# Hymba-style layer: sample rows and the first sparse keys emitted among the last forgetting-attention blocks, two small copies issued by GpSimd

## The chip, the cores and the metric

The kernel runs on one core of a Trainium2 chip. The metric is device time in microseconds of one execution; the times shown are three executions, and the profile is one further execution of the same program. Engines are named as in the profile: PE (TensorE), PEld (its weight loads), DVE (VectorE), ACT (ScalarE), POOL (GpSimd), SP (SyncE, which here only issues DMAs).

## The reference, cut to what matters

One inference step of one layer. A prompt of 1,024 tokens and 64 sample tokens (8 rows of a batch, 8 tokens each, with 512 cached tokens a row in pages) go through one input projection, whose columns feed two groups of 8 heads. Then:

```python
# group A, sparse attention: compressed, selected and window branches, gated
oa = gates[..., 0:1] * o_c + gates[..., 1:2] * o_s + gates[..., 2:3] * o_w
# group B, forgetting attention: softmax with a per-head decay bias
s = einsum('bqhd,bkhd->bhqk', q, k) * HEAD_DIM ** -0.5 + (cq - ck)
ob = einsum('bhqk,bkhd->bqhd', masked_softmax(s, k_pos <= q_pos), v)
y = x + concat(oa * silu(za), ob * silu(zb)) @ w_out
```

The sample rows do the same with their cached pages (selected-block, window and forgetting pages) in front of the new tokens. With 1,024 tokens and 16 blocks the selected branch covers all causal blocks, so both prompt attentions are dense causal ones; the window branch sees 512 tokens back.

## The kernel before, in words

Values are split in a high and a low 16-bit part, so a product takes two or three matmuls. The work runs in this order, with overlaps: the input projection in 15 chunks of columns; forgetting attention ("fox") over 8 heads, each in two halves of 512 queries; sparse attention ("nsa") over 8 tiles of 128 queries; the 8 sample rows; the output projection.

A fox half is `fox_attend` (lines 762 to 789): for each key block, two matmuls to a score bank (L774, L775), a mask (L777), the exponent on ACT (L711), its high part on ACT (L714), its low part on DVE or, every fifth time, POOL (L716), and the product with the values on PE (L724 to L726). `fox_max` (L757) finds the row maxima ahead of each half; it reads `km` and `qm`, which SP's queue copies from `k1` and `q1` (L703, L704). The first six heads have the last chunks of the input projection as filler between blocks; the last three halves ((6,1), (7,0), (7,1)) come after it and are emitted without filler.

A sparse tile is `nsa_tile`: `nsa_keys` and `nsa_queries` of the next tile (load `kn` or `nq` by SP, scale and split on ACT and POOL, transpose on PE, copy out of PSUM on ACT to `k1a` or `nq1`, then a DMA from there to `kma` (L1035) or `nqm` (L1051)), `nsa_max` (L1073 to L1088), `nsa_attend` (L1117 to L1125) and `nsa_compressed`. A sample row b is `sample_nsa`, `sample_nsa_out`, `sample_fox` and `sample_fox_out` (L1264 to L1371): page loads by SP (0.5 + 0.5 MB for nsa, 2 MB for fox), transposes (L1276, L1334), scores (L1284, L1344), softmax, product (L1304, L1360). It is cut into steps; `fill(rate)` pulls `rate` steps on average after each key block.

Each engine runs its instructions in the order in which they stand in its queue and waits on semaphores. That order is not the order of the text: a scheduler inside the tile framework places instructions by its own estimate of time, with program order and `high_priority` as the preference. A tile's memory comes from pools; a pool that takes over the memory of another (`SC.close()`) makes its first writers wait until the last readers of the old tiles are done. Before, `kma` and `k1a` lie in memory that the fox tiles hold to the end.

Of the kernel before, what the change touches and what calls it, by code (L numbers as in the profile page):

```python
# [22 lines left out]
NT = 8  # L23
T = 1024
# [69 lines left out]
def layer_kernel(ctx, tc, a, o):  # L94
# [633 lines left out]
    def put_max(m, rows, q, cols):  # L728

        n = m.shape[1]  # L730
        mh = B2.tile([128, 2, n], F16, name="mh")
# [15 lines left out]
    def fox_max(h, c):  # L747
        i = h % 2
        mst = B2.tile([128, 2, 4], F32, name="mst")
        m = mst[:, c]  # L750
        for x in range(4):
            t = 4 * c + x
            for s in range(c + 1):
                k0, k1_ = 4 * s, min(4 * s + 4, t + 1)
                n = (k1_ - k0) * 128
                p = PM.tile([128, 512], F32, name=bank["smax"][0], bufs=bank["smax"][1])
                nc.tensor.matmul(p[:, :n], qm[i][0:67, t * 128:(t + 1) * 128], km[i][0:67, k0 * 128:k0 * 128 + n],  # L757
                                 start=True, stop=True)
# [235 lines left out]
    C6 = S3.enter_context(tc.tile_pool(name="nsc", bufs=1, reuse_waits="tile"))  # L994
    BE = B3 = S3.enter_context(tc.tile_pool(name="nsl", bufs=1, reuse_waits="tile"))
    B2 = BN
    cvb = B3.tile([128, 130], F32, name="cvb")
    nc.gpsimd.memset(cvb, 0.0)
    for g in range(2):
        nc.scalar.activation(cvb[64 * g:64 * g + 63, 65 * g:65 * g + 65], cv_p[:, g], AF.Copy)  # L1000
# [4 lines left out]
    nc.gpsimd.memset(kmc, 0.0)  # L1005
    nc.gpsimd.memset(k1c, 0.0)
    stair = BN.tile([128, NT, 64], BF16, name="stair", bufs=1)
    nc.gpsimd.dma_start(stair, a["c_stair"])
    nc.sync.dma_start(kma[64:88].rearrange("p k n -> p (k n)"), a["c_kind"][:, 0:4 * T])
    for g in range(2):  # L1010
        nc.sync.dma_start(kmc[64:88, g, 64 * g:64 * g + 64], a["c_kind"][:, 4 * T:4 * T + 64])
    stairt = B3.tile([128, T], BF16, name="stairt")
    nc.gpsimd.dma_start(stairt, a["c_stairt"])

    def turned(t):
        return PM.tile([128, 512], F16, name="smax", bufs=SMAX)
# [4 lines left out]
        nc.gpsimd.tensor_sub(lo, src, hi)  # L1021

    def nsa_keys(t):
        ks = B2.tile([128, 4, 128], F16, name="nks", bufs=1)
        kn = B2.tile([128, 4, 64], F32, name="kn")
        nc.sync.dma_start(flat(kn[:, 0:2]), outs["slc"][0][t * 128:(t + 1) * 128, 0:128])
        nc.sync.dma_start(flat(kn[:, 2:4]), p_win[(t - 4) * 128:(t - 3) * 128, 0:128] if t >= 4 else kpark[t])
        split16(kn, nsc[:, 0:1], ks[:, :, 0:64], ks[:, :, 64:128])
        p = turned(t)
        for i in range(4):  # L1030
            nc.tensor.transpose(p[:, i * 128:(i + 1) * 128], ks[:, i], ident16)
        pk = p.rearrange("p (i n) -> p i n", i=4)
        c = slice(t * 128, (t + 1) * 128)
        nc.scalar.activation(k1a[:, :, c], pk, AF.Copy)
        nc.sync.dma_start(kma[0:64, :, c], k1a[0:64, :, c])  # L1035

    def nsa_queries(t):
        q = B2.tile([128, 8, 64], F32, name="nq", bufs=1)
        nc.sync.dma_start(q.rearrange("p h d -> p (h d)"), qpark[t])
        qsp = B2.tile([128, 8, 128], F16, name="nqs", bufs=1)  # L1040
        split16(q, nsc[:, 1:2], qsp[:, :, 64:128], qsp[:, :, 0:64])
        r = []
        for g in range(2):
            p = turned(t)
            for i in range(4):
                nc.tensor.transpose(p[:, i * 128:(i + 1) * 128], qsp[:, 4 * g + i], ident16)
            q1 = B2.tile([128, 512], F16, name="nq1", bufs=4)
            qm = B2.tile([128, 512], F16, name="nqm", bufs=4)
            nc.gpsimd.memset(qm[64:88], 0.0)
            nc.scalar.activation(q1, p, AF.Copy)  # L1050
            nc.sync.dma_start(qm[0:64], q1[64:128])  # L1051
            r.append((q1, qm))
        return r

    def nsa_max(g, t, qm):
        m = B2.tile([128, 3, 4], F32, name="nm")
        m2 = B2.tile([128, 2, 4], F32, name="nm2")
        for k in range(2):
            lo = 0 if k == 0 else max(0, t - 4)
            rem = (t + 1 - lo) % 4  # L1060
# [29 lines left out]
        put_max(m.rearrange("p k r -> p (k r)"), 64, qm, slice(0, 512))  # L1090

    def nsa_branch(po, k, g, t, oa):
        l = B2.tile([128, 2, 4], F32, name="nl")
# [38 lines left out]
    def nsa_compressed(t, qq, oa):  # L1132
# [26 lines left out]
    qq = nsa_queries(0)  # L1159
    csp = BN.tile([64, 2, 128], F16, name="csp", bufs=1)  # L1160
    nc.vector.memset(csp, 0.0)
    split16(ck_p, nsc[0:63, 0:1], csp[0:63, :, 0:64], csp[0:63, :, 64:128])
    p = turned(0)
    for g in range(2):
        nc.tensor.transpose(p[:, g * 64:(g + 1) * 64], csp[:, g], ident16[0:64, 0:64])
    for g in range(2):
        z = slice(64 * g, 64 * g + 64)
        nc.scalar.activation(k1c[:, g, z], p[:, z], AF.Copy)
        nc.scalar.activation(kmc[0:64, g, z], p[0:64, z], AF.Copy)
    nsa_keys(0)  # L1170
    nsa_max(0, 0, qq[0][1])
    nsa_max(1, 0, qq[1][1])


    S5 = ctx.enter_context(ExitStack())
# [245 lines left out]
    early[0] = False  # L1421
    rate = 1.5
    mixed[0] = 1
    for t in range(5):
        qq = nsa_tile(t, qq)
    for _ in filler:
        pass
# [188 lines left out]
```

## Time and profile before

| | |
|---|---|
| median of 3 executions | 989.49 us (984.81 to 993.89) |
| the profiled execution, its own time | 983.02 us |
| its span, first to last instruction | 981.2 us |
| mean granted PE clock | 0.984 |
| busy in the span | PE 907.3 us (92%), DVE 636.7 (65%), ACT 611.9 (62%), POOL 383.7 (39%) |
| chain that ended last | PE 68%, DVE 8%, DMA 7%, ACT 5%, issue 3%, POOL 3% |

Busy time is a sum over the whole span. The table of stretches among the rows further down gives it for a part of the span: the length of a stretch less PE's busy time is what PE stood idle there. The profile's PEclk is the granted clock as a share of full speed (1.00 is the level of 2.4 GHz, 0.5 that of 1.2 GHz; a value between is a mix over the stretch).

### The profile page before, as it was taken

To read this page: it belongs to the slowest core of one execution; us is meant where nothing else is said; L and a number is where in the kernel's file an instruction comes from. 1 tells how busy PE (TensorE), PEld (TensorE's weight loads), DVE (VectorE), ACT (ScalarE), POOL (GpSimd) and SP (SyncE) were. 2 spreads that over 40 slices of the span, in tenths; PEclk is the share of its full clock that TensorE was granted. 3 is DMA by queue.
4 is the path that set the end of the run, shared out by engine and by line. 5 is a ranking of instruction groups with operands and counts; after the bars stand their busy time and mean duration, and the time that the engine had idled before them with its cause. 6 is when DMAs were issued, how large, how long until landed. Compare 5 with 4: busy or idle time off the path is not lost.

```text
span 981.2 us, 24638 instructions
## 1 busy us (share of the span) xinstructions
PE 907.3 (92%) x9097; PEld 709.6 (72%) x9097; DVE 636.7 (65%) x1843; ACT 611.9 (62%) x1328; POOL 383.7 (39%) x546
## 2 busy tenths in 40 slices
PE   4898999999999999999997879889999988999997
PEld 3687889878888988877885546556666655677775
DVE  5764666664555426778777736878777888777461
ACT  6854643433454655797876677778898967455430
POOL 4544657754676333343414112334232246311000
PEclk9999999999999999999999999999999999999999
DMA  7563323332333432242215636455345333332241
GB/s 264 141 152 103 94 72 99 108 64 62 98 116 100 127 96 80 88 130 58 76 43 138 194 81 192 155 163 176 120 132 170 97 104 101 97 102 84 85 130 65
DMA packets 122425, 111.74 MB, mean 114 GB/s; under 512 B 39144, under 2 KB 103312, under 8 KB 122280
## 3 DMA queue, kind: packets, MB, share of 16 engines
q1 hardware_dynamic: 121296, 108.52, 37.1%
q0 software_dynamic: 576, 1.05, 0.6%
q8 instruction: 71, 1.16, 0.5%
q10 hardware_dynamic: 432, 0.59, 0.2%
q14 instruction: 50, 0.41, 0.1%
HBM read 79.57 MB, written 27.41 MB: 109 GB/s over the span
## 4 chain that ended last, share of the span: by engine, by line
PE 68%; DVE 8%; DMA 7%; ACT 5%; issue 3%; POOL 3%; SPq 1%; ACTq 0%; DVEq 0%; POOLq 0%
PE acc L245 25%; PE ctr L1502 7%; PE sa L474 3%; PE acc L238 3%; PE pv L724 2%; PE pv L726 2%; PE pv L725 2%; PE st L1117 2%; PE smax L1073 2%; PE st L1118 2%; DMA wst<-in_w_in_dram 2%; PE smax L757 1%; PE st L774 1%; PE ctr L1550 1%; PE st L775 1%
## 5 line engine op out<-in xcount | busy, mean ns | idle before, releaser
L245 PE MATMUL acc<-wsp,xth 128*128 128x256 f16 (+1 forms) x1920 | 335.0, 275 | 5.9 <-ACT xth L175 3.2
L245 PE MATMUL acc<-wsp,xtl 128*128 128x256 f16 (+1 forms) x960 | 264.2, 275 | 0.0
L245 PEld LDWEIGHTS <-xth 128*128 128x128 f16 x1920 | 187.0, 99 | 34.8 <-ACT xth L175 3.8
L1122 ACT ACTIVATE pf<-st,nsc 128x512 f32<-128x512 f32 x132 | 98.8, 781 | 35.2 <-PE st L1118 16.8
L245 PEld LDWEIGHTS <-xtl 128*128 128x128 f16 x960 | 94.5, 98 | 14.8 <-issue 1.4
L724 PEld LDWEIGHTS <-phi 128*128 128x128 f16 x816 | 77.3, 97 | 17.7 <-issue 5.5
L726 PEld LDWEIGHTS <-plo 128*128 128x128 f16 x816 | 77.2, 100 | 11.5 <-DVE plo L716 2.9
L725 PEld LDWEIGHTS <-phi 128*128 128x128 f16 x816 | 77.3, 98 | 3.2 <-issue 0.5
L1123 ACT ACTIVATE phi<-pf 128x1024 f16<-128x1024 f32 (+1 forms) x76 | 71.5, 951 | 12.9 <-PE pv L725 8.0
L711 ACT ACTIVATE pf<-st,nsc 128x512 f32<-128x512 f32 (+1 forms) x96 | 62.9, 669 | 16.0 <-PE st L777 5.8
L1125 DVE TENSOR_TENSOR plo<-pf,phi 128x1024 f16<-128x1024 f32 (+1 forms) x56 | 64.8, 1159 | 8.9 <-ACT phi L1123 8.7
L264 POOL TENSOR_TENSOR nss<-nss,nhalf 128x4 f32<-128x4 f32 (+3 forms) x72 | 68.4, 950 | 4.4
L1125 POOL TENSOR_TENSOR plo<-pf,phi 128x1024 f16<-128x1024 f32 (+1 forms) x20 | 37.2, 1859 | 77.4 <-ACT phi L1123 71.6
L716 DVE TENSOR_TENSOR plo<-pf,phi 128x512 f16<-128x512 f32 (+3 forms) x77 | 51.9, 680 | 22.2 <-ACT phi L714 20.3
L724 PE MATMUL pv<-va,phi 128*128 128x65 f16 x528 | 60.0, 194 | 3.7 <-DVE nt L1102 1.8
L201 ACT ACTIVATE vsq<-wst 128x512 f16<-128x512 f32 (+2 forms) x72 | 40.2, 560 | 33.6 <-DMA wst<-in_w_in_dram 32.9
L725 PE MATMUL pv<-va,phi 128*128 128x64 f16 x528 | 59.9, 196 | 0.0
L726 PE MATMUL pv<-va,plo 128*128 128x65 f16 x528 | 57.5, 193 | 0.2 <-POOL plo L1125 0.2
L714 ACT ACTIVATE phi<-pf 128x512 f16<-128x512 f32 (+1 forms) x96 | 48.7, 523 | 7.8 <-PE pv L726 6.5
L1073 PE MATMUL smax<-kma,nqm 88*128 88x512 f16 (+3 forms) x192 | 48.9, 314 | 4.8 <-DVE nm L1082 2.0
L744 DVE CUSTOM_DVE_ANT_0 junk<-smax,maskw,nm 128x512 bf16<-128x512 f32 x64 | 47.7, 746 | 6.3 <-PE smax L1073 4.1
L1117 PE MATMUL st<-nqm,kma 88*128 88x512 f16 x132 | 50.2, 380 | 0.5 <-ACT pf L1122 0.4
(454 smaller groups left out, 2352.4 us busy)
## 6 DMA issues: line engine op xcount, KB each, us to landing
wst<-in_w_in_dram SPq DMA_DIRECT2D x56, 256.0 KB
sfk<-in_cache_fox_kv_dram SPq DMA_DIRECT2D x32, 256.0 KB
sfv<-in_cache_fox_kv_dram SPq DMA_DIRECT2D x32, 256.0 KB
out_dram<-kv SPq DMA_DIRECT2D x52, 128.0 KB
xin<-in_x_prompt_dram SPq DMA_DIRECT2D x8, 512.0 KB
cpair<-in_cache_nsa_cmp_kv_dram SPq DMA_DIRECT2D x64, 64.0 KB
zpark<-z SPq DMA_DIRECT2D x32, 128.0 KB
spg<-in_cache_nsa_slc_kv_dram SPq DMA_DIRECT2D x32, 128.0 KB
```

The source lines that it names most:

```text
L245: nc.tensor.matmul(ps[:, :n], x[:, k, t * 128:(t + 1) * 128], w[k // 2][:, i, k % 2, :n], start=(k == 0 and j == 0), stop=(k == KT - 1 and ...
L264: nc.gpsimd.tensor_tensor(ss[:n, 0, :h], ss[:n, 1, :h], nhalf[:n, :h], op=ALU.pow)
L711: nc.scalar.activation(p[:n, :cols], ps[:n, :cols], AF.Exp, bias=nsc[:n, 3:4], scale=nsc[:n, 6:7])
L724: nc.tensor.matmul(po[:, s, 0:65], hi[:, c], v[:, 0:65], start=f, stop=False, skip_group_check=True)
L725: nc.tensor.matmul(po[:, s, 0:64], hi[:, c], v[:, 65:129], start=False, stop=False, skip_group_check=True)
L726: nc.tensor.matmul(po[:, s, 0:65], lo[:, c], v[:, 0:65], start=False, stop=l, skip_group_check=True)
L1073: nc.tensor.matmul(pr[:, r], qm[0:88, (r0 + r) * 128:(r0 + r + 1) * 128], kma[0:88, 2 * k + g, j0 * 128:j1 * 128], start=r == 0, stop=not ...
L1117: nc.tensor.matmul(ps, kma[0:88, 2 * k + g, c], qm[0:88], start=True, stop=False)
L1122: nc.scalar.activation(pf[:, 512 * x:512 * x + 512], ps, AF.Exp, bias=nsc[:, 3:4], scale=nsc[:, 2:3])
L1123: nc.scalar.activation(hi[:, 0:n], pf[:, 0:n], AF.Copy)
L1125: (nc.gpsimd if turn[0] % share[mixed[0]] == 0 else nc.vector).tensor_sub(lo_[:, 0:n], pf[:, 0:n], hi[:, 0:n])
L1502: nc.tensor.matmul(ps, l[:, k], w[:, k, c], start=(k == 0 and j == 0), stop=(k == KT - 1 and j == 2))
```

## The change

Four things. (1) The last three fox halves are no longer emitted first at high priority: the sample constants and the first two sample steps come ahead of them, then 0.9 sample steps are pulled after each of their 20 key blocks, and also after each block of the sparse tiles (1.5 before). (2) The keys and queries of sparse tile 0 (`nsa_first`) are emitted behind half (6,1), their maxima behind `fox_early(7)`, ahead of half (7,1). For that `kma`, `k1a` and the small tiles move to pools on the side of memory that is free when the input projection ends. (3) The copies to `kma` and `nqm`, and three loads of constants, are issued by POOL instead of SP. (4) Four sparse tiles, not five, are emitted ahead of the output weights. Two score banks that sample steps borrowed at first are no longer borrowed.

```diff
-        put_max(m, 96, qm[i], slice(512 * c, 512 * c + 512))
+        put_max(m, 96, qm[i], slice(512 * c, 512 * c + 512), B2)
...
+    C6 = ctx.enter_context(tc.tile_pool(name="nsc", bufs=1, side="right", reuse_waits="tile"))
...
-    with tc.high_priority(offset=250):
-        fox_attend(6, 1)
-        fox_early(7)
-        fox_attend(7, 1)
-    SC.close()
...
-    nc.sync.dma_start(kma[64:88].rearrange("p k n -> p (k n)"), a["c_kind"][:, 0:4 * T])
...
-        nc.sync.dma_start(kma[0:64, :, c], k1a[0:64, :, c])
+        nc.gpsimd.dma_start(kma[0:64, :, c], k1a[0:64, :, c])
...
-            nc.sync.dma_start(qm[0:64], q1[64:128])
+            nc.gpsimd.dma_start(qm[0:64], q1[64:128])
...
+    def nsa_first():
+        nc.gpsimd.memset(kmc, 0.0)
+        nc.gpsimd.memset(k1c, 0.0)
+        nc.gpsimd.dma_start(kma[64:88].rearrange("p k n -> p (k n)"), a["c_kind"][:, 0:4 * T])
...
+        nsa_keys(0)
+        qq = nsa_queries(0)
...
-        if early[0] and early[1] % 5 in (1, 3):
-            return PM.tile([128, 512], F32, name="st", bufs=2)
...
-    for _ in range(3):
-        next(filler)
-    rate = 1.5
+    rate = 0.9
+    for _ in range(2):
+        next(filler)
+    fox_attend(6, 1)
+    qq = nsa_first()
+    fox_early(7)
+    for g in range(2):
+        nsa_max(g, 0, qq[g][1])
+    fox_attend(7, 1)
+    SC.close()
...
-    for t in range(5):
+    for t in range(4):
         qq = nsa_tile(t, qq)
...
-    for t in range(5, NT):
+    for t in range(4, NT):
         qq = nsa_tile(t, qq)
```

Up to the first blocks of half (6,1) the order on PE is the same. Three places show what moves after that. In the changed kernel every line from `nsa_first` on has a lower number (L1334 is L1317, L1073 is L1054, L1035 is L1016, L1051 is L1032).

SP's queue in half (6,1), where the copies of head 7's `km` and `qm` stand. `spg`, `sfk` and `sfv` are sample pages, `kn` and `nq` inputs of sparse tiles. Before:

```order
L788 DMA obpark<-obt 128x4x128
L703 DMA km_5787<-k_5789 64x1024
L1271 DMA spg<-in_cache_nsa_win_kv_dram 128x4x256
L1026 DMA kn<-out_dram 128x128
L704 DMA qm_5788<-q_5790 64x1024
L1027 DMA kn<-kpark 128x128
L1039 DMA nq<-qpark 128x512
```

The same place in the changed kernel (left out: four more page loads of the kind shown):

```order
L1254 DMA spg<-in_cache_nsa_win_kv_dram 128x4x256
L1308 ISA
L1308 DMA sfk<-in_cache_fox_kv_dram 128x512
L1311 ISA
L1311 DMA sfv<-in_cache_fox_kv_dram 128x512
...
L788 DMA obpark<-obt 128x4x128
L703 DMA km_5787<-k_5789 64x1024
L1279 DMA out_dram<-spg 120x256
L1280 DMA out_dram<-spg 128x3x256
L1308 ISA
L1308 DMA sfk<-in_cache_fox_kv_dram 128x512
L704 DMA qm_5788<-q_5790 64x1024
```

Six page loads of 256 KB now stand ahead of both copies, and a seventh with two stores of the window pages ahead of the second.

PE where the first sparse maxima stand. Before, behind the last product of half (7,1):

```order
L726 MATMUL pv<-vb_5089,plo 128x65
L1259 MATMUL ctr<-ident,spr 128x128 x4
L1334 MATMUL ctr<-ident,sfk 128x128 x4
L1262 MATMUL st<-ident,spr 128x128
L1334 MATMUL ctr<-ident,sfk 128x128 x4
L1073 LDWEIGHTS nqm
L1073 MATMUL smax<-kma,nqm 128x128
```

Changed, between the maxima of half (7,1) (L735) and its first scores (L774):

```order
L1242 MATMUL ctr<-ident,spr 128x128 x4
L1245 MATMUL ctr<-ident,spr 128x128
L1259 MATMUL ctr<-ident,spg 128x128 x4
L735 LDWEIGHTS mh
L735 MATMUL smax<-ident_62,mh 8x128
L1054 LDWEIGHTS nqm
L1054 MATMUL smax<-kma,nqm 128x128
...
L774 LDWEIGHTS km_5787
L774 MATMUL st<-qm_5788,km_5787 128x512
```

The first sparse maxima moved ahead of a whole fox half.

POOL in the same stretch, `plo` being the low part of a fox block, `nks` and `nqs` splits for sparse tiles. Before:

```order
L1021 TENSOR_TENSOR nqs<-nq,nqs 128x8x64
L1021 TENSOR_TENSOR nks<-kn,nks 128x4x64
L716 TENSOR_TENSOR plo<-pf,phi 128x256
L716 TENSOR_TENSOR plo<-pf,phi 128x512 x2
L1021 TENSOR_TENSOR nqs<-nq,nqs 128x8x64
L716 TENSOR_TENSOR plo<-pf,phi 128x512
```

Changed:

```order
L716 TENSOR_TENSOR plo<-pf,phi 128x512
L1231 MEMSET spr 128x64
L1016 DMA kma<-k1a 64x4x128
L1002 TENSOR_TENSOR nks<-kn,nks 128x4x64
L1032 DMA nqm<-nq_9724 64x512
L1032 DMA nqm<-nq_9734 64x512
L1002 TENSOR_TENSOR nqs<-nq,nqs 128x8x64
L716 TENSOR_TENSOR plo<-pf,phi 128x512
```

A fox block's low part now stands behind three copies, each of which waits for a copy by ACT. In all, 8 copies to `kma`, 16 to `nqm` and 3 loads go from SP's queue to POOL's.

## Rows read from the trace of the kernel before

**Rows 1.** Busy by stretch: stretch, length, PE, PEld, DVE, ACT, POOL, PEclk, DMA, GB/s.

```profile
536.00:545.00 9.00, 8.39 (x81) 5.35 (x82) 5.52 (x17) 7.48 (x15) 0.67 (x1) 0.69 0.54 147
545.00:555.00 10.00, 8.84 (x122) 6.13 (x121) 5.88 (x19) 7.72 (x17) 1.16 (x1) 1.00 1.01 317
555.00:578.00 23.00, 18.10 (x170) 10.37 (x170) 11.89 (x31) 16.92 (x37) 4.77 (x5) 0.85 0.24 74
578.00:591.00 13.00, 8.99 (x94) 6.17 (x92) 5.83 (x16) 6.28 (x18) 0.87 (x3) 1.00 0.49 122
600.00:700.00 100.00, 88.90 (x1066) 61.02 (x1065) 75.31 (x241) 77.98 (x162) 32.70 (x42) 0.98 0.54 168
700.00:780.00 80.00, 77.83 (x1007) 52.97 (x1006) 66.27 (x183) 72.87 (x144) 24.12 (x29) 1.00 0.45 143
780.00:860.00 80.00, 72.42 (x707) 48.08 (x705) 66.47 (x152) 50.36 (x76) 36.13 (x28) 0.98 0.30 92
```

**Rows 2.** Timeline of PE: start us, us, engine, line, operation [idle before <-releaser].

```profile
536.38 0.27 PE L735 MATMUL smax<-ident,mh 128*8 128x128 f16 x1 [5.25 <-DVE mh L733]
548.43 0.33 PE L757 MATMUL smax<-km,qm 67*128 67x128 f16 x2
548.69 0.68 PE L1227 MATMUL ctr<-ones,slp 128*64 128x64 f32 x8
594.77 0.19 PE L724 MATMUL pv<-va,phi 128*128 128x65 f16 x1
606.34 0.87 PE L1334 MATMUL ctr<-ident,sfk 128*128 128x128 f32 x6 [0.95 <-DMA sfk<-in_cache_fox_kv_dram]
687.41 0.38 PE L1138 MATMUL st<-nqm,kmc 88*128 88x512 f16 x1 [2.05 <-ACT pf L1122]
```

**Rows 3.** Timeline of DVE, the one long instruction near 531 us.

```profile
531.08 4.10 DVE L716 TENSOR_TENSOR plo<-pf,phi 128x256 f16<-128x256 f32 x1
```

**Rows 4.** The chain of waits in order of time, its DMA pieces: start us, us, what.

```profile
541.92 4.96 DMA spg<-in_cache_nsa_win_kv_dram
550.25 5.49 DMA sfv<-in_cache_fox_kv_dram
555.76 3.88 DMA kn<-kpark
606.09 3.50 DMA nq<-qpark
682.38 3.51 DMA nq<-qpark
```

**Rows 5.** Timeline of SP's queue, one issue.

```profile
543.23 0.49 SPq L704 DMA_DIRECT2D qm<-q  x1
```

**Rows 6.** SP's queue, waits from 500 to 800: total us, times, longest.

```profile
SPq L1035 <- ACT nks L1020: 14.7, 5, 4.2
SPq L1051 <- ACT nq L1050: 11.8, 3, 8.2
```

**Rows 7.** The chain of waits, four pieces of sample work on PE.

```profile
585.50 1.02 PE ctr L1304 x14
597.97 0.89 PE ctr L1360 x26
600.75 1.01 PE ctr L1284 x4
634.18 1.14 PE ctr L1334 x8
```

**Rows 8.** Timeline of POOL, a DMA issue, and the first operation behind an idle stretch.

```profile
522.27 0.79 POOL L1008 DMA_DIRECT2D stair<-in_c_stair_dram  x1
527.60 0.42 POOL L1021 TENSOR_TENSOR csp<-ck_p,csp 63x128 f16<-63x128 f32 x1 [2.59 <-ACT csp L1020]
```

**Rows 9.** DMA view, issues on POOL's queue: count, KB each, us to landing.

```profile
spread<-in_c_spread_dram POOLq DMA_DIRECT2D x1, 512.0 KB, 5.0
stair<-in_c_stair_dram POOLq DMA_DIRECT2D x1, 128.0 KB, 3.4
```

More of the change, by code (lines that the diff above doesn't have):

```diff
@@ L726, in pv, with put_max @@
             nc.tensor.matmul(po[:, s, 0:65], lo[:, c], v[:, 0:65], start=False, stop=l, skip_group_check=True)
-    def put_max(m, rows, q, cols):
+    def put_max(m, rows, q, cols, pool):
         n = m.shape[1]
-        mh = B2.tile([128, 2, n], F16, name="mh")
+        mh = pool.tile([128, 2, n], F16, name="mh")
         nc.vector.tensor_scalar(mh[:, 0], m, 1.0 / MSCALE, None, op0=ALU.mult)
@@ L984, in layer_kernel @@
     BN = ctx.enter_context(tc.tile_pool(name="nsw", bufs=2, side="right", reuse_waits="tile"))
+    C6 = ctx.enter_context(tc.tile_pool(name="nsc", bufs=1, side="right", reuse_waits="tile"))
     PS = ctx.enter_context(tc.tile_pool(name="ps3", bufs=1, space=PSUM, reuse_waits="tile"))
     SMAX, PV, CTR = 2, 1, 3
-    with tc.high_priority(offset=250):
-        fox_attend(6, 1)
-        fox_early(7)
-        fox_attend(7, 1)
-    SC.close()
-    S3 = ctx.enter_context(ExitStack())
[L994 to L1000, printed above, removed]
+    S3 = ctx.enter_context(ExitStack())
     kma = C6.tile([128, 4, T], F16, name="kma")
@@ L1004, in layer_kernel @@
     k1c = BN.tile([128, 2, 128], F16, name="k1c", bufs=1)
-    nc.gpsimd.memset(kmc, 0.0)
-    nc.gpsimd.memset(k1c, 0.0)
     stair = BN.tile([128, NT, 64], BF16, name="stair", bufs=1)
-    nc.gpsimd.dma_start(stair, a["c_stair"])
-    nc.sync.dma_start(kma[64:88].rearrange("p k n -> p (k n)"), a["c_kind"][:, 0:4 * T])
[L1010 to L1013, printed above, removed]
     def turned(t):
@@ L1023, in nsa_keys @@
     def nsa_keys(t):
-        ks = B2.tile([128, 4, 128], F16, name="nks", bufs=1)
-        kn = B2.tile([128, 4, 64], F32, name="kn")
+        ks = BN.tile([128, 4, 128], F16, name="nks", bufs=1)
+        kn = BN.tile([128, 4, 64], F32, name="kn")
         nc.sync.dma_start(flat(kn[:, 0:2]), outs["slc"][0][t * 128:(t + 1) * 128, 0:128])
@@ L1034, in nsa_keys @@
         nc.scalar.activation(k1a[:, :, c], pk, AF.Copy)
-        nc.sync.dma_start(kma[0:64, :, c], k1a[0:64, :, c])
+        nc.gpsimd.dma_start(kma[0:64, :, c], k1a[0:64, :, c])
     def nsa_queries(t):
-        q = B2.tile([128, 8, 64], F32, name="nq", bufs=1)
+        q = BN.tile([128, 8, 64], F32, name="nq", bufs=1)
         nc.sync.dma_start(q.rearrange("p h d -> p (h d)"), qpark[t])
-        qsp = B2.tile([128, 8, 128], F16, name="nqs", bufs=1)
+        qsp = BN.tile([128, 8, 128], F16, name="nqs", bufs=1)
         split16(q, nsc[:, 1:2], qsp[:, :, 64:128], qsp[:, :, 0:64])
@@ L1046, in nsa_queries @@
                 nc.tensor.transpose(p[:, i * 128:(i + 1) * 128], qsp[:, 4 * g + i], ident16)
-            q1 = B2.tile([128, 512], F16, name="nq1", bufs=4)
-            qm = B2.tile([128, 512], F16, name="nqm", bufs=4)
+            q1 = BN.tile([128, 512], F16, name="nq1", bufs=4)
+            qm = BN.tile([128, 512], F16, name="nqm", bufs=4)
             nc.gpsimd.memset(qm[64:88], 0.0)
             nc.scalar.activation(q1, p, AF.Copy)
-            nc.sync.dma_start(qm[0:64], q1[64:128])
+            nc.gpsimd.dma_start(qm[0:64], q1[64:128])
             r.append((q1, qm))
@@ L1055, in nsa_max @@
     def nsa_max(g, t, qm):
-        m = B2.tile([128, 3, 4], F32, name="nm")
-        m2 = B2.tile([128, 2, 4], F32, name="nm2")
+        m = BN.tile([128, 3, 4], F32, name="nm")
+        m2 = BN.tile([128, 2, 4], F32, name="nm2")
         for k in range(2):
@@ L1089, in nsa_max @@
         nc.vector.tensor_reduce(out=m[:, 2], in_=pr, axis=AX.X, op=ALU.max)
-        put_max(m.rearrange("p k r -> p (k r)"), 64, qm, slice(0, 512))
+        put_max(m.rearrange("p k r -> p (k r)"), 64, qm, slice(0, 512), BN)
     def nsa_branch(po, k, g, t, oa):
-        l = B2.tile([128, 2, 4], F32, name="nl")
+        l = BN.tile([128, 2, 4], F32, name="nl")
         nc.vector.reciprocal(l[:, 1], po[:, :, 64])
@@ L1146, in nsa_compressed @@
                 nc.tensor.matmul(po[:, r].rearrange("p g d -> p (g d)"), pc[:, c:c + 128], cvb, start=True, stop=True)
-            l = B2.tile([128, 2, 4], F32, name="nl")
+            l = BN.tile([128, 2, 4], F32, name="nl")
             lv = [l[:, x].rearrange("p (r g) -> p r g", r=2) for x in range(2)]
@@ L1157, in nsa_compressed @@
             nc.gpsimd.tensor_tensor(dst[:, 0], dst[:, 0], tmp, op=ALU.add)
[L1159 to L1172, printed above, removed]
+    def nsa_first():
[3 more added lines that the diff above has]
+        for g in range(2):
+            nc.gpsimd.dma_start(kmc[64:88, g, 64 * g:64 * g + 64], a["c_kind"][:, 4 * T:4 * T + 64])
+        nc.gpsimd.dma_start(stair, a["c_stair"])
+        nsa_keys(0)
+        qq = nsa_queries(0)
+        csp = BN.tile([64, 2, 128], F16, name="csp", bufs=1)
+        nc.vector.memset(csp, 0.0)
+        split16(ck_p, nsc[0:63, 0:1], csp[0:63, :, 0:64], csp[0:63, :, 64:128])
+        p = turned(0)
+        for g in range(2):
+            nc.tensor.transpose(p[:, g * 64:(g + 1) * 64], csp[:, g], ident16[0:64, 0:64])
+        for g in range(2):
+            z = slice(64 * g, 64 * g + 64)
+            nc.scalar.activation(k1c[:, g, z], p[:, z], AF.Copy)
+            nc.scalar.activation(kmc[0:64, g, z], p[0:64, z], AF.Copy)
+        return qq
     S5 = ctx.enter_context(ExitStack())
@@ L1418, in layer_kernel @@
     quota[0] = 0.0
-    for _ in range(3):
+    rate = 0.9
+    for _ in range(2):
         next(filler)
-    early[0] = False
-    rate = 1.5
+    fox_attend(6, 1)
+    qq = nsa_first()
+    fox_early(7)
+    for g in range(2):
+        nsa_max(g, 0, qq[g][1])
+    fox_attend(7, 1)
+    SC.close()
+    BE = B3 = S3.enter_context(tc.tile_pool(name="nsl", bufs=1, reuse_waits="tile"))
+    cvb = B3.tile([128, 130], F32, name="cvb")
+    nc.gpsimd.memset(cvb, 0.0)
+    for g in range(2):
+        nc.scalar.activation(cvb[64 * g:64 * g + 63, 65 * g:65 * g + 65], cv_p[:, g], AF.Copy)
+    stairt = B3.tile([128, T], BF16, name="stairt")
+    nc.gpsimd.dma_start(stairt, a["c_stairt"])
     mixed[0] = 1
-    for t in range(5):
+    for t in range(4):
         qq = nsa_tile(t, qq)
```

2 lines of the change are left out of this document (removed).

## The prediction, as it was put on record before the changed kernel ran

> **What bounds the kernel now.** I read the table of stretches first, then PE's timeline in the stretches where PE stands idle, then the chain of waits there, then SP's and POOL's queues. PE is the bound: it is busy 907.3 of 981.2 us. The first table shows where it is not [rows 1]: length less PE's busy time gives 0.6, 1.2, 4.9 and 4.0 us of idle in the four stretches from 536 to 591, 10.7 in all; 11.1 from 600 to 700; 2.2 from 700 to 780; 7.6 from 780 to 860. In the last but one of these, where sparse tiles and sample rows run mixed, idle is only 2.7% of the stretch: that is what this kernel can do when there is other work for PE. From 536 to 591 there is less: the last three fox halves and the start of the sparse part run alone, and ACT is idle there too (38.4 us busy of 55). So what the change can win is idle on PE; the matmuls stay the same in number.
>
> Why is PE idle there? The chain from 541.9 to 559.6 goes through three DMAs one behind the other: a window page, a fox page, a key tile for the sparse part [rows 4]. The sample pages share SP's queue with the small loads, and ACT takes its scaling of the key tile in order, so a late key tile holds the exponents behind it. The stretch from 545 to 555 moves 317 GB/s with the DMA engines full [rows 1].
>
> **The change, part by part.** I set a ledger on PE from 536.38, where its order is still the same, to the first sparse product, 594.77 [rows 2]: 58.4 us, of which 10.7 idle. Up to the same product, the changed order holds more sample work. Counted there: 16 more transposes of fox pages at 1.14 us for 8, 2.3 us; 16 more fox value products, recorded twice each, 32 at 0.89 for 26, 1.1; 8 more nsa value products, also recorded twice, 16 at 1.02 for 14, 1.2; 2 more score products, 4 records, 1.0 [rows 7]. The rest (17 more transposes and some small products, less two compressed products and nine value products) I put at 0.9 from the same transposes. Sum 6.5 us of PE work brought forward. Without any idle the point would come at 594.8 - 10.7 + 6.5 = 590.6, and everything behind it would have 6.5 us less to do: a gain of 10.7 less the idle I that stays or comes new.
>
> I from both sides. Below: the 2.7% of the mixed stretch, on 57 us, 1.5. Above: all 10.7 as before, and more if the page loads hurt. To the 1.5 I add one wait. The copy of head 7's `qm` is issued at 543.23 and first used at 548.43 [rows 2, 5]. Six page loads of 256 KB now go ahead of the copies in the queue, 1.57 MB, which at 317 GB/s [rows 1] is 5.0 us. Of this the copy's slack covers 1.7 (5.2 us to its use, less about 3.5, as the small loads in the chain land [rows 4]), and the sample work that now stands ahead of the use covers 1.8 (0.7 for the decay sums of L1227 [rows 2] and 1.1 for eight page transposes at the pace of those in rows 7). Left: 1.5. The upper bound takes the seventh load and the two stores too, 2.35 MB or 7.4 us, and a copy issued 1 us later: 6.6. I take 1.5, since the pages start earlier than before and some will have drained. So I = 3.0 and **the first term is -7.7**.
>
> Not changed: PE's longest stop, 5.25 us ahead of 536.38 [rows 2]. It ends with a DVE instruction of 4.10 us [rows 3], whose like takes 0.4; POOL's row of splits and memsets just there is the same in the changed order but for the swap of two. The three constant loads added to POOL's queue stand before it, in an idle 2.59 us ahead of `csp` [rows 8]. I cost this at nothing; if the cover fails, the stop grows by up to 3 x 0.79 [rows 8], 2.4.
>
> Sparse tiles with sample rows, 600 to 780. SP's queue stood 14.7 us waiting to issue `kma`, 11.8 for `nqm` [rows 6]; all that time no page was requested. These issues leave SP. Two query loads (3.50 and 3.51 us in the chain [rows 4]) were late behind such waits, and PE's stops that go with them are 0.95 and 2.05 us [rows 2]. The queries of tiles 1 and 2 are now loaded while fox runs. I take these two, **-3.0**. Bounds: nothing, and all 13.3 us of idle there less 2.7% of 180, which is 8.4.
>
> POOL gets 27 issues. One costs 0.79 us there [rows 8], 21 us over some 280, on an engine with 67 of 100 and 56 of 80 us free [rows 1]: nothing, except where a copy itself is waited for. A DMA from POOL's queue landed after 3.4 us for 128 KB and 5.0 for 512 KB [rows 9]; from SP's the chain's small loads took 3.5 to 3.9 [rows 4]. A 64 KB copy between two tiles of SBUF is in neither list; I put it next to the 3.4, so no difference. Bounds: 1 us less each, since it is no longer behind pages, to 1.6 more.
> The Trainium skill speaks against this part. "DMA: Bandwidth & Descriptors", section "SWDGE vs HWDGE vs iDMA", gives plain copies to SP or ACT and says that GpSimd writes its descriptors into a ring in SBUF, from which VectorE can lock it out; its section "Latency and other measured facts" has 0.6 us to the first byte on SP's path and 1 us on GpSimd's. By that an estimate of 0.4 us for each of 14 copies that tiles 1 to 7 wait for would make the sum 5.6 worse. No row here separates the two paths.
>
> Five to four tiles ahead of the output weights: between 780 and 860 PE idles 7.6 us [rows 1] around the weights' loading. The order of tile 4 against the weights is swapped, both are needed: nothing, with 4 us either way. From 860 PE is full to the last 20 us, so what is won before should arrive at the end.
>
> **Sum.** -7.7 - 3.0 = -10.7 against the profiled execution's 983.0, 972.3. That execution stands 6.5 us under the median of 989.49, so the forecast for the median is 978.8, about **979**, 1.1% less. About 1% (9.9 us) is what a measurement of this kernel can tell from no change.
>
> **The rivals.** First, *more is won*: I = 1.5 and the sparse tiles reach 8.4, a gain of 17.6, with 2 from the weights 19.6: 970. For it: PE's clock was 0.85 from 555 to 578 [rows 1], after stops that would be gone; against it: ACT is busy 91% from 700 to 780, so the mixed stretch has a second bound close by.
>
> Second, *POOL's copies take back the gain*. Each is behind a wait for ACT in an in-order queue, with low parts of fox or sparse blocks behind it, and may land 1.6 us later (5.0 against 3.4 [rows 9]). Seven tiles at 1.6 are 11.2, of which other work hides perhaps a fifth: 979 + 9 = 988, no change. This is also how the skill's rule on the descriptor ring would come out. For it: DVE and POOL do disturb each other here [rows 3]. Against: POOL's landings shown are not slow.
>
> Third, on the other side, *the pages ahead of everything small*. SP's queue is one line and PE's order is fixed: if the copy of `qm`, then the queries of tile 1 on ACT, then keys and queries of tile 2 and the next row's pages each come 5.0 to 5.5 us late, as the pieces in the chain do [rows 4], then I = 1.5 + 4 x 5.1, about 22, and the sparse tiles win nothing: 11 us slower, 1000. It decides from I = 10.7, where the gain is gone; it takes three of the four to be uncovered. For it: the DMA engines were full from 545 to 555 already, and more pages are asked for there now. Against: the pages also start about 4 us earlier, and kept SP waiting less.
>
> Fourth, *the gain does not reach the end*: the weights' loading from 780 on stays where it was, and PE idles there instead: 985.
>
> **Chances.** The forecast 0.45, with a range of its own of 974 to 984; more is won 0.16; POOL's copies 0.16; not to the end 0.08; slower 0.15. Faster by over 1% (below 979.6) holds a little over half of the forecast and the first rival: 0.43. Within 1%: the rest of the forecast, the second and the fourth: 0.42. Slower: 0.15. The range from 969 to 992 leaves out the third rival and a tail of the first.
>
> **What would show it.** In the changed profile: the first sparse product near 594 with the fox products of sample row 0 and the nsa products of row 1 done before it; PE's idle between 536 and that point near 3 us; the first `fox_max` of head 7 waiting for its `qm` copy by 1 to 2 us; no query load in the chain from 600 to 700; copies on POOL's queue landing in about 3.5 us; the sample rows ending about 10 us earlier. Wrong would be: idle of 10 us or more before the first sparse product with DMAs as releasers (third rival), PE or ACT waiting for POOL's copies in each tile (second), or the same end of the stretch to 860 in spite of sample rows that end earlier (fourth).

## The result, and the profile after

The changed kernel takes 975.5 us (median of 4 executions, 974.53 to 976.02), the kernel before 989.72 beside it: ratio 0.9857, 95% interval 0.9811 to 0.9903, so 1.4% faster. The forecast was 979. The profiled execution took 974.53 us, with a span of 972.8 and a mean granted clock of 0.988; PE is busy 901.1 us in it (907.3 before).

The stretches of [rows 1] in the changed kernel (stretch, length, PE, PEld, DVE, ACT, POOL, PEclk, DMA, GB/s):

```profile
536.00:545.00 9.00, 7.61 (x81) 5.08 (x82) 5.33 (x17) 7.62 (x15) 1.02 (x2) 0.81 0.94 291
545.00:555.00 10.00, 8.09 (x79) 5.36 (x78) 3.49 (x11) 6.72 (x14) 1.15 (x1) 0.90 0.88 282
555.00:578.00 23.00, 20.08 (x234) 13.54 (x235) 13.87 (x47) 17.17 (x47) 5.01 (x8) 0.89 0.32 95
578.00:591.00 13.00, 13.00 (x176) 9.36 (x168) 9.02 (x24) 11.25 (x25) 2.28 (x4) 1.00 0.60 198
591.00:600.00 9.00, 7.22 (x76) 4.52 (x74) 5.05 (x11) 8.12 (x22) 4.69 (x8) 1.00 0.71 162
600.00:700.00 100.00, 91.05 (x1117) 62.88 (x1114) 83.95 (x268) 81.78 (x165) 39.69 (x54) 0.98 0.52 161
700.00:780.00 80.00, 76.16 (x1034) 51.57 (x1034) 66.50 (x166) 69.51 (x133) 22.45 (x29) 1.00 0.37 114
780.00:860.00 80.00, 72.99 (x649) 48.70 (x647) 69.59 (x147) 49.85 (x72) 38.99 (x32) 1.00 0.34 115
```

Length less busy PE time is 1.4, 1.9, 2.9 and 0 us from 536 to 591 (6.2, before 10.7); 1.8 from 591 to 600 (before 0.1); 9.0 from 600 to 700 (before 11.1); 3.8 from 700 to 780 (before 2.2); 7.0 from 780 to 860 (before 7.6). The span became 8.4 us shorter, but PE's idle in these stretches only 3.8. Over the whole span PE's idle fell by 2.2 us (73.9 to 71.7) and its busy time by 6.2, though its matmuls are the same in number.

PE's timeline in the changed kernel, against [rows 2]:

```profile
536.36 0.27 PE L735 MATMUL smax<-ident,mh 128*8 128x128 f16 x1 [4.86 <-DVE mh L733]
551.99 0.34 PE L757 MATMUL smax<-km,qm 67*128 67x128 f16 x2 [1.91 <-DMA qm<-q]
599.38 0.19 PE L724 MATMUL pv<-va,phi 128*128 128x65 f16 x1
773.52 0.27 PE L1353 MATMUL ctr<-ident,son 128*64 128x128 f32 x1
```

The start of the ledger is at the same time, and the first sparse product at 599.38 instead of 594.77. The ledger's stretch in both traces, the kernel before and then the changed one:

```profile
536.38:594.77 58.39, 48.01 (x488) 30.10 (x489) 31.54 (x90) 41.40 (x94) 8.13 (x12) 0.90 0.48 141
```

```profile
536.36:599.38 63.02, 55.38 (x624) 37.30 (x625) 35.84 (x104) 50.30 (x118) 14.07 (x21) 0.92 0.60 181
```

Idle up to that product fell from 10.4 us (the prediction's 10.7 is that of the stretches from 536.00 to 591) to 7.6, and 7.4 us more of PE's busy time lie ahead of it. The sample rows end at 773.5; their last transpose, the same operation, stood at 786.22 before.

Two pieces of the chain of waits (start us, us, what), against [rows 4]:

```profile
546.00 5.94 DMA qm<-q
...
608.26 4.67 DMA sfv<-in_cache_fox_kv_dram
612.95 4.03 DMA kn<-out_dram
```

Head 7's `qm` copy is now a piece of the chain; the query loads are gone from it between 600 and 700. A key load stands at the same place as before (there 612.34, for 3.08 us), now behind a sample page. In SP's queue (total us, times, longest, 500 to 800), against [rows 6]:

```profile
SPq L1311 <- PE ctr L1343: 40.2, 7, 9.4
SPq L1308 <- PE ctr L1317: 30.4, 6, 6.8
SPq L1007 <- POOL nks L1002: 13.3, 3, 10.2
```

The 26.5 us that SP waited for ACT ahead of the two copies are gone, but the queue waits instead for buffers of sample pages (L1311, before 27.7) and for a split on POOL.

The new issues on POOL (count, KB each, median us to landing), beside [rows 9]:

```profile
nqm<-nq POOLq DMA_DIRECT2D x16, 64.0 KB, 3.1
kma<-k1a POOLq DMA_DIRECT2D x8, 64.0 KB, 4.0
```

### The profile page after: what moved, and what is told of

Read it like the earlier page. It is cut to its first block, busy times and chain, and to the rows that moved or that the text cites. A ratio compares the mean times of both kernels' runs of the same rounds, so it can differ in the third digit from the quotient of the medians.

```text
span 972.8 us, 24636 instructions
## 1 busy us (share of the span) xinstructions
PE 901.1 (93%) x9097; PEld 707.1 (73%) x9097; DVE 644.9 (66%) x1845; ACT 612.3 (63%) x1328; POOL 397.4 (41%) x571
## 3 DMA queue, kind: packets, MB, share of 16 engines
q0 software_dynamic: 1456, 2.83, 1.3%
## 4 chain that ended last, share of the span: by engine, by line
PE 64%; DVE 9%; DMA 7%; ACT 6%; issue 3%; POOL 2%; SPq 1%; DVEq 0%; ACTq 0%; POOLq 0%
PE acc L245 22%; PE ctr L1499 7%; PE sa L474 3%; PE acc L238 3%; PE smax L1054 2%; PE pv L726 2%; PE pv L724 2%; PE pv L725 2%; PE st L1098 2%; PE st L1099 2%; DMA wst<-in_w_in_dram 2%; DVE junk L744 2%; PE ctr L1547 1%; PE st L774 1%; PE st L775 1%
## 5 line engine op out<-in xcount | busy, mean ns | idle before, releaser
L245 PEld LDWEIGHTS <-xtl 128*128 128x128 f16 x960 | 94.5, 98 | 14.8 <-issue 1.4
L1104 ACT ACTIVATE phi<-pf 128x1024 f16<-128x1024 f32 (+1 forms) x76 | 71.7, 948 | 14.0 <-PE pv L726 8.8
L1106 DVE TENSOR_TENSOR plo<-pf,phi 128x1024 f16<-128x1024 f32 (+1 forms) x58 | 67.0, 1158 | 10.8 <-ACT phi L1104 10.0
L1106 POOL TENSOR_TENSOR plo<-pf,phi 128x1024 f16<-128x1024 f32 (+1 forms) x18 | 34.6, 1923 | 51.4 <-ACT phi L1104 40.6
L714 ACT ACTIVATE phi<-pf 128x512 f16<-128x512 f32 (+1 forms) x96 | 48.7, 524 | 10.3 <-PE pv L726 8.8
L1054 PE MATMUL smax<-kma,nqm 88*128 88x512 f16 (+3 forms) x192 | 49.1, 316 | 3.8 <-DVE nm L744 3.5
L1084 POOL TENSOR_TENSOR oa<-oa,nt 128x256 f32<-128x256 f32 x22 | 19.7, 894 | 78.8 <-DVE nt L1083 65.0
```

The source lines that it names most:

```text
L245: nc.tensor.matmul(ps[:, :n], x[:, k, t * 128:(t + 1) * 128], w[k // 2][:, i, k % 2, :n], start=(k == 0 and j == 0), stop=(k == KT - 1 and ...
L1054: nc.tensor.matmul(pr[:, r], qm[0:88, (r0 + r) * 128:(r0 + r + 1) * 128], kma[0:88, 2 * k + g, j0 * 128:j1 * 128], start=r == 0, stop=not ...
L1104: nc.scalar.activation(hi[:, 0:n], pf[:, 0:n], AF.Copy)
L1106: (nc.gpsimd if turn[0] % share[mixed[0]] == 0 else nc.vector).tensor_sub(lo_[:, 0:n], pf[:, 0:n], hi[:, 0:n])
```

## The experiments

Each run gives its length (span) and its mean granted clock. Length times (1 - clock) is what the half clock would have cost had PE been busy all that time; it is called lost length here. Means over the runs; "before" is the kernel before, run beside each of the three groups of experiments; the first runs of the changed kernel stood beside others of it (989.72), so kernels of different groups are best compared by their ratios.

| kernel | ratio (95%) | runs | length | clock | lost length |
|---|---|---|---|---|---|
| before | 1 | 50 | 985.4 | 0.977 | 22.3 |
| changed, and changed_again | 0.9857 (0.9811 to 0.9903), 0.9885 (0.9849 to 0.9921) | 8 | 974.0 | 0.986 | 13.3 |
| copies_on_sp, and again | 0.9839 (0.9782 to 0.9897), 0.9859 (0.9828 to 0.9890) | 8 | 970.1 | 0.984 | 15.3 |
| no_fill_in_fox | 0.9878 (0.9847 to 0.9909) | 4 | 972.4 | 0.985 | 15.1 |
| fill_only | 0.9893 (0.9864 to 0.9922) | 4 | 974.8 | 0.985 | 14.4 |
| queue_only | 0.9998 (0.9969 to 1.0027) | 10 | 984.3 | 0.979 | 21.0 |
| neither | 0.9913 (0.9887 to 0.9939) | 10 | 976.9 | 0.986 | 13.5 |
| keys_early_only | 0.9868 (0.9836 to 0.9900) | 4 | 971.4 | 0.985 | 14.8 |
| own_banks_only | 0.9888 (0.9848 to 0.9927) | 5 | 975.1 | 0.988 | 11.7 |
| neither_shared_banks | 0.9958 (0.9927 to 0.9988) | 11 | 981.3 | 0.978 | 22.0 |
| keys_early_shared_banks | 0.9981 (0.9953 to 1.0009) | 11 | 984.2 | 0.977 | 22.4 |
| five_tiles_copies_on_sp | 0.9903 (0.9873 to 0.9933) | 8 | 976.8 | 0.986 | 14.2 |

### The parts as the prediction saw them

**copies_on_sp**, from the changed kernel:

```diff
-        nc.gpsimd.dma_start(kma[0:64, :, c], k1a[0:64, :, c])
+        nc.sync.dma_start(kma[0:64, :, c], k1a[0:64, :, c])
-            nc.gpsimd.dma_start(qm[0:64], q1[64:128])
+            nc.sync.dma_start(qm[0:64], q1[64:128])
```

> The changed kernel, with the copies of `kma` and `nqm` issued on SP again. If SP's queue was the cost (the prediction's second term, 3.0 us), the time goes from 975.5 to about 978.5, and loads of queries come back into the chain of waits between 600 and 720. If the copies on GpSimd cost something instead (the second rival, 1 to 1.6 us in each of seven tiles), it falls to 965 to 970. Within 2 us of 975.5 the queue of these copies does not matter.

Measured: 969.05 us, no loss and perhaps a gain. The query loads are back in its chain (`nq<-qpark` at 612.82 and 702.47, 3.64 us each), as expected, and it costs nothing. The second term of the sum is not there in the changed kernel.

**no_fill_in_fox**, from the changed kernel:

```diff
-    rate = 0.9
-    for _ in range(2):
-        next(filler)
+    rate = 0.0
...
+    for _ in range(3):
+        next(filler)
+    rate = 1.5
-    for t in range(4):
+    for t in range(5):
```

> The changed kernel without sample steps among the last fox halves: they start after them at rate 1.5 and five tiles stand ahead of the output weights, as in the kernel before; the first sparse keys stay early, the copies stay on GpSimd. If filling PE's idle among the fox halves is most of the gain (the prediction's first term, 7.7 us), the time is 983 or more, with 10 us of PE idle again ahead of the first sparse product. If the early keys or the queue carry the gain, it stays within 3 us of 975.5.

Measured: 973.86 us, so almost the whole gain stays. This seemed to leave the first term to the early keys; it did not, as the later runs show.

**fill_only**, from the changed kernel:

```diff
-    qq = nsa_first()
     fox_early(7)
-    for g in range(2):
-        nsa_max(g, 0, qq[g][1])
     fox_attend(7, 1)
+    qq = nsa_first()
+    for g in range(2):
+        nsa_max(g, 0, qq[g][1])
```

> The changed kernel with the first sparse keys, queries and maxima emitted after the last fox half instead of among the fox halves; the filling and the queue stay. If the filling alone carries the first term, the time stays within 2 us of 975.5. If the early keys matter as much (the key tile, its copies and the first maxima are a chain of DMAs with nothing left to cover it), the idle comes back behind the last fox half: three DMAs of 3.5 to 5 us one behind the other, partly covered by sample steps, 4 to 8 us, 980 to 984.

Measured: 976.64 us, most of the gain too. Either move "alone" gives 1.1 to 1.2%, both 1.2 to 1.4%. This pointed to a cause that they share, but fill_only is not without early keys. Its first sparse maximum stands ahead of the last fox product, whatever the order in the text:

```profile
574.50 0.40 PE L1054 MATMUL smax<-kma,nqm 88*128 88x128 f16 x4 [0.23 <-DMA nqm<-nq]
588.30 0.19 PE L726 MATMUL pv<-vb,plo 128*128 128x65 f16 x1
```

**queue_only**, from the kernel before: the edit of copies_on_sp the other way round.

> The kernel before, with only the copies of `kma` and `nqm` moved from SP's queue to GpSimd's. If they held back the query loads (the prediction's second term), it is 3 us faster than the kernel before, ratio 0.997; if they cost on GpSimd, it is 4 to 11 us slower, ratio 1.004 to 1.011; if neither, ratio 1.000 with PE's idle from 600 to 700 near 11 us as before.

Measured: 986.48 us against 986.24, ratio 0.9998, with 13.3 us of PE idle from 600 to 700. In the kernel before, the queue of the copies is worth nothing that can be measured; the interval, 0.9969 to 1.0027, leaves room for 3 us either way.

### What the moves share

**changed_again** is the changed kernel, unedited.

> The changed kernel as it is, on the chip of the three runs beside it, as their measure. Its ratio to the kernel before was 0.9857; the same is expected, 0.982 to 0.990.

Measured: 975.73 us, ratio 0.9885.

**copies_on_sp_again** repeats copies_on_sp.

> The changed kernel with the copies of `kma` and `nqm` on SP's queue, once more beside the changed kernel itself. If GpSimd's queue takes some of the gain back, it is 3 to 6 us faster than the changed kernel in the same session, as the first look suggested (0.9839 against 0.9857, each with its own runs of the kernel before); if the queue is worth nothing either way, as in the kernel before (0.9998), within 2 us.

Measured: 973.62 us, 2.1 below changed_again, between the two expectations. In mean length it is 2.3 us, give or take 2.5. (The table's 970.1 and 974.0 are 3.9 apart, but half of those runs stood beside different runs of the kernel before, 986.24 and 989.72.) That GpSimd's queue costs something in the changed kernel is likely, and not shown.

**neither**, from the changed kernel: the edits of no_fill_in_fox and fill_only together.

> The changed kernel with neither of its two moves: no sample steps among the last fox halves, the first sparse keys, queries and maxima behind the last half, five tiles ahead of the output weights. What stays of the change: the tiles of the sparse part stand in other memory, the fox halves have no raised priority, the copies go through GpSimd. Each move alone gave nearly all of the gain (0.9878 and 0.9893). If the two are two covers for the same waits, this kernel is back at the kernel before, ratio 0.997 to 1.003. If the gain of both came from what they share (priority, memory), it keeps most of it, ratio 0.988 to 0.992.

Measured: 977.71 us, ratio 0.9913, so most of the gain is left with both moves undone in the text of the program. But the first sample score product in its trace still stands ahead of the last fox half's end, and so does the first sparse maximum:

```profile
553.24 0.64 PE L1267 MATMUL ctr<-skt,qbs 128*64 128x512 f32 x1
572.80 0.40 PE L1054 MATMUL smax<-kma,nqm 88*128 88x128 f16 x4 [1.27 <-DMA nqm<-nq]
585.30 0.19 PE L726 MATMUL pv<-vb,plo 128*128 128x65 f16 x1
```

The scheduler has brought both forward by itself. no_fill_in_fox and neither were not without filling, and fill_only and neither not without early keys; their names promise what the runs did not do.

**keys_early_only**, from no_fill_in_fox: the edit of copies_on_sp as well.

> The changed kernel without sample steps among the fox halves and with the copies on SP's queue: the early keys alone. If early keys take the chain of DMAs out of the place between the last fox half and the first sparse tile, and that is the gain, it stays near the kernel without filling (ratio 0.988), and the filling adds 0 to 3 us to it. If the filling brings more once the copies are on SP (0.984 with it), it is 4 us slower than the kernel with both.

Measured: 973.67 us, like no_fill_in_fox. Here, too, the scheduler fills in.

### The banks

What let the scheduler do it? In the kernel before, the first three sample steps take two of every five PSUM tiles from `st`, the pair of banks of the fox scores, and tiles of one name get their banks in the order of the text. PE's timeline there:

```profile
573.84 0.22 PE L774 MATMUL st<-qm,km 104*128 104x128 f16 x1 [0.42 <-ACT pf L711]
574.81 0.65 PE L1276 MATMUL st<-ident,spg 128*128 128x128 f32 x4 [0.21 <-ACT pf L711]
576.98 1.33 PE L1284 MATMUL st<-skt,qbs 128*64 128x512 f32 x4
578.33 0.19 PE L726 MATMUL pv<-vb,plo 128*128 128x65 f16 x1
```

The sample tiles in `st` (L1276, L1284) come right behind the last fox score (L774), and all sample work behind them waits with them.

**own_banks_only**, from the kernel before:

```diff
-    early = [True, 0]
+    early = [False, 0]
```

> The kernel before with one thing of the change: sample tiles no longer take two of five PSUM banks from the fox scores' pair (`st`), only their own three (`ctr`). The kernel without both moves still had sample score products among the fox halves; what held them back in the kernel before was that the first such tile takes a bank of `st` behind all fox scores. If that is the filling of the prediction's first term, this one line gives what the kernel without both moves had: ratio 0.990 to 0.993, sample products ahead of the last fox product, the granted clock 0.985 or more against 0.978. If that gain came from the moved memory or the dropped priority, it is at 1.000.

Measured: 976.56 us, ratio 0.9888: one line gives what the whole change gave in changed_again (0.9885; 0.9857 in its first runs). The product that stood at 576.98 now stands at 551.12, in a bank of `ctr`; the first sparse maximum comes later than the last fox product, and the first sparse product at 603.53:

```profile
551.12 1.07 PE L1284 MATMUL ctr<-skt,qbs 128*64 128x512 f32 x2
580.19 0.19 PE L726 MATMUL pv<-vb,plo 128*128 128x65 f16 x1
589.41 0.58 PE L1073 MATMUL smax<-kma,nqm 88*128 88x128 f16 x4 [2.83 <-DMA kma<-k1a]
603.53 0.19 PE L724 MATMUL pv<-va,phi 128*128 128x65 f16 x1
```

So this kernel has filling and no early keys, and even a new wait of 2.83 us for the late key copy. Its gain goes with the clock: the mean rose from 0.977 to 0.988 and lost length fell by 10.6 us, the length by 10.3.

**neither_shared_banks**, from neither (the two lines of the kernel before are put back; early keys by the scheduler, since the moved memory allows them, but no filling):

```diff
+    early = [True, 0]
...
+        early[1] += 1
+        if early[0] and early[1] % 5 in (1, 3):
+            return PM.tile([128, 512], F32, name="st", bufs=2)
```

> The kernel without both moves, but with the sample tiles taking their first banks from the fox scores' pair again: now no sample score stands ahead of the last fox half, and what is left of the change is the memory, the priority and the queue. By the theory of the banks it is at the kernel before, ratio 0.998 to 1.002; by the rival (memory or priority) it stays at 0.991.

Measured: 981.62 us, ratio 0.9958, between the two: the banks account for 0.45% of the 0.87% that neither won, and 0.42% stay, each give or take 0.3 to 0.4%. The clock is back at 0.978. Its first sparse maximum stands at 569.25, ahead of the last fox product, so its sparse keys are early although the text puts them behind; which of this, the memory and the priority gives the rest was not separated. The next run has all three as well and keeps only 0.19%, so the rest itself is uncertain.

**keys_early_shared_banks**, the same edit on no_fill_in_fox.

> The first sparse keys early, no sample steps among the fox halves and the fox scores' banks shared again, so that the sample scores stay behind the last fox half too: the early keys truly alone (copies on GpSimd). If they cover the chain of DMAs by themselves, ratio 0.993 to 0.995, a gain of 5 to 7 us that shows as PE idle removed ahead of the first sparse product. If they only help where sample work fills in as well, 0.998 to 1.002.

Measured: 985.74 us, ratio 0.9981: early keys without filling give nothing that can be measured (at most 0.5% by the interval). The stretch behind the last fox halves in this trace, and then in that of no_fill_in_fox, whose only difference is the banks:

```profile
550.00:600.00 50.00, 42.12 (x411) 27.60 (x409) 29.22 (x77) 34.88 (x78) 12.48 (x19) 0.80 0.34 94
```

```profile
550.00:600.00 50.00, 44.15 (x517) 29.63 (x517) 34.39 (x95) 40.77 (x99) 13.45 (x21) 1.00 0.48 145
```

PE is busy for nearly as long in both (42.1 and 44.2 us), but with the shared banks part of the stretch runs at 1.2 GHz (clock 0.80) and gets 411 matmuls done, with own banks all of it at 2.4 GHz and 517. Over all traces the clock of this stretch is 0.93, 0.90, 0.93 and 0.80 in the four kernels with shared banks, and 0.90 to 1.00, with a mean of 0.96, in the ten others. One stretch of one execution does not carry the gain, though: own_banks_only is the one of the ten at 0.90, below the kernel before.

Three pairs of kernels differ in the banks alone. Own banks gain 1.12% (own_banks_only against the kernel before), 0.45% (neither) and 1.03% (no_fill_in_fox), and lost length falls by 10.6, 8.5 and 7.3 us. The busy times over the span from four profile pages, two with shared banks (the kernel before, keys_early_shared_banks) and two with own banks (own_banks_only, no_fill_in_fox):

```profile
PE 907.3 (92%) x9097; PEld 709.6 (72%) x9097; DVE 636.7 (65%) x1843; ACT 611.9 (62%) x1328; POOL 383.7 (39%) x546
PE 913.6 (93%) x9097; PEld 713.6 (72%) x9097; DVE 640.1 (65%) x1843; ACT 613.7 (62%) x1328; POOL 393.9 (40%) x573
PE 905.4 (93%) x9097; PEld 708.2 (73%) x9097; DVE 641.6 (66%) x1843; ACT 613.4 (63%) x1328; POOL 386.6 (40%) x546
PE 903.5 (93%) x9097; PEld 709.8 (73%) x9097; DVE 639.7 (66%) x1843; ACT 611.8 (63%) x1328; POOL 400.4 (41%) x573
```

PE has the same 9,097 matmul records in all 14 traces. With shared banks (four traces) it is busy 910.1 us on the mean and idle 72.5, with own banks (ten) busy 903.5 and idle 69.5. Of the 9.6 us between, 6.6 are busy time and 3.0 idle. (The kernel before and own_banks_only are only 1.9 us of busy time apart here, since the former's profile ran at a clock of 0.984, far above its mean.)

**five_tiles_copies_on_sp**, from copies_on_sp:

```diff
-    for t in range(4):
+    for t in range(5):
```

> The changed kernel with its copies on SP's queue and five tiles ahead of the output weights instead of four, the sample rate the same. The prediction took the fifth tile for nothing, with 4 us either way. By that, ratio 0.984 to 0.988 as with four tiles. If four tiles matter because the sample rows' end fits them, it is 3 us or more slower, 0.989 or above.

Measured: 979.13 us, ratio 0.9903. The mean length is 6.7 us above that of the 8 runs with four tiles, give or take 3.4; the kernel before was 1.0 longer beside it, so 5.7. no_fill_in_fox (0.9878) and keys_early_only (0.9868) have five tiles as well, at a rate of 1.5, and are not slower than the changed kernel, so five tiles seem to cost only at a rate of 0.9. The stretches from 700 on, with five tiles and then with four (copies_on_sp_again):

```profile
700.00:780.00 80.00, 74.09 (x993) 50.47 (x992) 66.79 (x174) 69.19 (x131) 23.70 (x27) 1.00 0.36 113
780.00:860.00 80.00, 73.43 (x674) 47.98 (x673) 66.02 (x142) 50.81 (x74) 35.85 (x28) 0.96 0.29 97
```

```profile
700.00:780.00 80.00, 75.58 (x1011) 51.57 (x1012) 65.11 (x175) 69.64 (x131) 22.75 (x25) 0.98 0.36 113
780.00:860.00 80.00, 75.13 (x675) 50.44 (x674) 64.60 (x149) 51.49 (x76) 37.60 (x29) 0.98 0.35 112
```

PE stands idle 12.5 us with five and 9.3 with four.

The lowest ratios found, 0.9839 and 0.9859, are those of copies_on_sp, the change with its two copies left on SP's queue; they are not clear of the changed kernel's.

## Why the prediction was right, and where not

The time and the sign were right, and so was the place: sample work between the last fox halves is what wins. own_banks_only shows it alone, and keys_early_shared_banks shows that the other move without it wins nothing that can be measured. That the sum came out so near the time is luck: its main terms were wrong in size, and what it left out made up for them. The steps:

**First term, -7.7: the place right, the size and what is saved wrong.** The step that failed is that the gain is PE's idle removed, with I = 3.0 left. I was 7.6. The wait for head 7's `qm`, put at 1.5, came as forecast: the copy was 5.94 us under way, and PE stopped for it at 551.99 for 1.91. (The upper bound given for it, 6.6, does not follow from its terms, 7.4 + 1 - 1.7 - 1.8 = 4.9; the sum does not use it.) The work brought forward was 7.4 us (6.5 forecast). What failed is the 2.7% share of the mixed stretch, 1.5 us: beside it and the wait for `qm`, 4.2 us of stops remain, those of over 0.4 us being 0.5 to 1.2 us each. Idle gave 2.7 us, not 7.7.

In its place stands PE's busy time, shorter by 6.6 us of 9.6 between the means of the traces with own and with shared banks, and it goes with the clock. The granted clock of the kernel before is 0.977 on the mean, of the changed kernel 0.986: lost length 22.3 and 13.3 us, 9.0 less, out of a mean gain of 11.4. Not all of the lost length is time, since PE may stand idle while the clock is low. Within the kernel before itself, the third of the 50 runs with the lowest clock has 26.1 us of lost length and a mean length of 988.0, the third with the highest 18.3 and 983.3: 4.7 us for 7.8, or 0.6 for one. By this, an estimate for the clock's part is 5.4 to 9 of the 11.4 us. No run here changed the clock alone, so this split stays open. The prediction had the row for it, PE's clock of 0.69 and 0.85 in [rows 1], and used it only as a point for the first rival. It also could not see the size: the profiled execution was the fastest of the kernel before that was shown, 983.0 against a median of 989.49, and only one of the 50 later runs has a higher clock than its 0.984.

The Trainium skill ("Perfetto Trace Analysis", section "Matmul Optimizations") says that PE's power follows its use, so that matmuls should be issued back to back. The runs agree on the mean: the clock is 0.977 to 0.979 in the four kernels whose sample matmuls wait behind the fox scores, and 0.984 to 0.988 in the others. The same section asks for all eight PSUM banks to be used. That rule does not cover what was found here: sample tiles that gave up two of five banks made the kernel 1.1% faster, since these banks were shared with work whose order they then fixed.

**A part not priced.** That two score banks are no longer borrowed stands among the changes described ahead of the prediction, and the sum has no term for it. It is the part that decides: the written filling adds 0.2% (neither 0.9913, fill_only 0.9893, and that with four tiles instead of five), which the intervals of 0.3% each do not tell from nothing.

**Second term, -3.0: wrong.** queue_only is at 0.9998, and copies_on_sp, with the query loads back in its chain, is no slower than the changed kernel. One of the two stops was misread: the 0.95 us ahead of 606.34 [rows 2] ended with a sample page, and the query load that it was put down to landed only at 609.59 (606.09 and 3.50, [rows 4]). The late query loads did leave the chain, as forecast, but SP's queue then waited longer for sample pages' buffers, and PE's idle from 600 to 780 stayed at 12.8 us (13.3 before). The wait ahead of the queue's head was replaced by the next one.

**POOL's copies, 0: perhaps a few us the other way.** The landing times were near the forecast, 3.1 and 4.0 us against 3.4. The kernel is faster with the copies on SP in all three comparisons (0.9839 against 0.9857, 0.9859 against 0.9885, and keys_early_only's 0.9868 against no_fill_in_fox's 0.9878), in none by more than its interval; in the closest one it is 2.3 us, give or take 2.5. So the second rival, at 9 us, has at most its sign. The Trainium skill ("DMA: Bandwidth & Descriptors", section "SWDGE vs HWDGE vs iDMA") gives plain copies to SP or ACT, and the prediction's estimate from that page was 5.6 us. The runs of the changed kernel lean in its direction, with less than its size; those of the kernel before show no cost. Where the time would go is open: no wait for a `kma` or `nqm` copy is among the ten largest of PE in the changed trace from 600 to 860.

**Four tiles, 0 with 4 either way: probably too small.** With the copies on SP and a rate of 0.9 it is 5.7 us, give or take 3.4, in favour of four.

**Right as forecast:** the stop ahead of 536 (5.25, now 4.86); the sample rows' earlier end (12.7 us, about 10 forecast); the fox products of sample row 0 and the nsa products of row 1 ahead of the first sparse product, though that came at 599.38, not near 594; and that what is won arrives at the end, so the fourth rival falls. The third falls too: of the small loads behind the pages only the `qm` copy stopped PE for more than 1.5 us ahead of the first sparse product. The first rival's way did not come either: I stayed at 7.6 and the sparse tiles' idle at 12.8, so that the gain is above the forecast for another reason. The forecast of 979 came out 3.5 us above the time because terms that were too large (idle by 5.0, queries by 3.0) and terms left out (the clock, four tiles, perhaps POOL's copies) nearly cancel.

## What to carry to other kernels

Before pricing what a move of code fills, look for what keeps the scheduler from making that move by itself: a buffer or a bank whose turns are given out in the order of the text can hold back all work behind it, and one line can free it. Read PE's granted clock over several runs, and its busy time beside its idle time, as a term of its own: filling work can leave the idle time nearly as it was and still win. And an experiment that undoes a move in the text has to be read in its trace first, since the schedule may make the move anyway.

## What the runs showed of the hardware

The same kernel's runs differ in mean clock from 0.969 to 0.985 (50 runs of the kernel before), and their length with it, from 992.7 to 978.4 us. In every trace here the clock falls to 1.2 GHz for a part of the time from 530 to 550 (0.74 to 0.83), around the stop of 4.9 to 5.3 us that ends between 532.8 and 539.1, whatever follows. A copy of 64 KB between two tiles of SBUF, issued by GpSimd, landed after 3.1 us (`nqm`) and 4.0 us (`kma`) on the median in the changed kernel, and after 2.6 and 2.9 us in queue_only.
